# Half of the q and k transposes of two attention mixers moved from TensorE to VectorE and a round trip through HBM, and one projection order for both mixers

## The chip, the cores and the metric

The kernel runs on one core of a Trainium2 chip. The metric is the device time of one execution in microseconds (us). A profile of one execution accompanies each time: it tells what each engine did when, on TensorE (PE for matmuls, PEld for its weight loads), VectorE (DVE), ScalarE (ACT), GpSimd (POOL) and SyncE (SP, which here only issues transfers).

## The reference

A decoder trunk of two layers over 256 positions and 1024 channels, 16 heads of 64, in float32. Each layer is an FFN half-step, an attention mixer and another FFN half-step, all on normed input:

```python
for layer in range(2):
    h = h + 0.5 * swiglu(rmsnorm(h, ffn1_norm[layer]), ...)
    hn = rmsnorm(h, mix_norm[layer])
    if layer == 0:
        h = h + mixer_a(hn, a_w_qkv, a_w_o, pos)          # q, k, v from hn
    else:
        h = h + mixer_b(hn, b_w_q, b_w_o, k, v, ...)      # k, v from shared_kv
    h = h + 0.5 * swiglu(rmsnorm(h, ffn2_norm[layer]), ...)
    if layer == 0:
        k, v = shared_kv(h, kv_norm, kv_w, pos)
return rmsnorm(h, final_norm)
```

In both mixers q and k get a partial rotary turn (the first 16 of each head's 64 channels). At 256 positions mixer a is causal attention with weights that count how many of three dilated windows hold a key, and mixer b is plain causal attention; the kernel does both with the same code and two masks.

## The kernel before

Every float32 operand is split into a high part (float32r, by ACT) and the rest (by DVE), and a product takes three matmuls: high x high, high x low, low x high. Weights stream from HBM through a ring of five raw tiles and are split on ACT and DVE (`wh_`, `wl_`) a few pieces ahead of TensorE. The FFNs fill most of the time; the change is in `mixer`, called once per layer ("a", then "b").

A mixer projects the 256 tokens in two halves t = 0, 1 of 128 (tokens on partitions). `segs` lists the projections in order: each is up to 512 columns wide, and runs through `product` (L188, L190, L192). The heads go in four groups g of four heads (256 columns). `evacuate` brings a projection out of PSUM with the norm's scale (`rt_`, L1091), `rotate` turns the first channels on DVE (L910 to L913), and values are split to `vs_`. When q and k of a group and half are there, `turn_in` turns them on TensorE: four transposes of 128x128 against an identity (L1080) into a PSUM tile `qt_`, then `parts_of` splits it into `qk_` (ACT L99, DVE L96). `scores` (matmuls `s_`, L931 to L939), a softmax over ACT, DVE and POOL (`sm_`, `nm_`, `ls_`), the transposes of the weights (`pt_`, L971), `values` (`po_`, L1002) and the output projection (`ot_`, L877 to L879) follow.

The order of all this is the order of the program, set by an `Agenda`: projections advance a clock by 0.68 per step, and follow-up calls are entered with a delay on that clock (`agenda.after(1.5, ...)`, `soon` is 0.7). `plan` gives, per group, the delays of scores (s), transposes (t) and values (v; vt also does the next pair's transposes). A scheduler then puts each engine's instructions in a row. Within an engine instructions run in that row, and SP's transfers too are issued in one row.

The two mixers have different orders. Mixer a projects q and k of a group together, each group in turn:

```python
    qk = [(n1, xs, [("q", w, g * n, n, g), ("k", w, H * DH + g * n, n, g)]) for g in range(NG)]
    v = [(n1, xs, [("v", w, 2 * H * DH + g * n, 2 * n, g)]) for g in (0, 2)]
    mixer("a", [qk[0], v[0], qk[1], qk[2], qk[3], v[1]],
```

Mixer b projects k and v of group 0, q of groups 0 and 1, k and v of group 1, k of groups 2 and 3, q of 2 and 3, v of 2 and 3.

The last stage of the kernel (after mixer b) already turns data by another route, for the residual stream: DVE transposes 32x32 blocks (`turned`, L1196), SP writes the pieces to HBM (L1201) and reads them back in another order (`h`, L1207).

Of the kernel before, what the change touches and what calls it, by code (L numbers as in the profile page):

```python
# [10 lines left out]
F32 = mybir.dt.float32  # L11
# [56 lines left out]
def trunk(ctx: ExitStack, tc: tile.TileContext, a: dict, out: bass.AP):  # L68
# [14 lines left out]
    def atile(shape, dt=F32, name="a"):  # L83
        return ap_.tile(shape, dt, tag="a", name=name)
# [4 lines left out]
    def flat(ap):  # L89
        return ap.rearrange("p c n -> p (c n)")  # L90

    def parts_of(hi, lo, src, scale=1.0, later=None):

        def rest():
            if isinstance(scale, float):
                return first, nc.vector.tensor_sub(lo, src, hi.bitcast(F32))  # L96
            return first, nc.vector.scalar_tensor_tensor(lo, src, scale, hi.bitcast(F32), op0=ALU.mult, op1=ALU.subtract)

        first = nc.scalar.activation(hi, src, AF.Copy, scale=scale)  # L99
        (later or (lambda call: call()))(rest)  # L100
# [4 lines left out]
    def trt(name):  # L105
        return trp.tile([P, 512], F32, tag="tr", name=name)
# [796 lines left out]
    def rotate(v, t, name):  # L903

        n = v.shape[1]
        cs = rot[:, t, 0:1, :].to_broadcast([P, n, ROT])
        sn = rot[:, t, 1:2, :].to_broadcast([P, n, ROT])
        ta = sp.tile([P, n, ROT], F32, tag="rota", name=f"ra_{name}", bufs=2)
        tb = sp.tile([P, n, ROT], F32, tag="rotb", name=f"rb_{name}", bufs=2)
        nc.vector.tensor_mul(ta, v[:, :, :ROT], cs)  # L910
        nc.vector.tensor_mul(tb[:, :, :HALF], v[:, :, HALF:ROT], sn[:, :, :HALF])
        nc.vector.tensor_mul(tb[:, :, HALF:], v[:, :, :HALF], sn[:, :, HALF:])
        nc.vector.tensor_add(v[:, :, :ROT], ta, tb)  # L913
# [116 lines left out]

        return scores, turn, values, values_on

    def mixer(name, segs, plan, wo, mask, after, queue={}, beside=(), idle={}):

        n = HG * DH
        blocks, heads, qks, vss = [], {}, {}, {}
        specs = []  # L1040
# [24 lines left out]
        scores, turn, values, values_on = attention(agenda, lambda g: (qks[g], vss.get(g)), mask, name, blocks, idle)

        def turns(p):
            for i in range(2):
                turn(p, i)

        def turn_in(g, t):

            if t == 0:
                qks[g] = ap_.tile([P, 2, 4, NT, P], F32R, tag="qk", name=f"qk_{name}{g}", bufs=2)
            tr = trt(f"qt_{name}{g}_{t}")
            for i, kind in enumerate("qk"):
                s = heads[kind, g, t].rearrange("p a b -> p (a b)")
                for k in range(2):
                    at = (2 * i + k) * P
                    nc.tensor.transpose(tr[:, at:at + P], s[:, k * P:(k + 1) * P], ident)  # L1080
            parts_of(*[qks[g][:, i, :, t, :] for i in range(2)], tr.rearrange("p (k n) -> p k n", n=P), later=agenda.soon)
            if t == NT - 1:
                for wait, step, p in plan[g]:
                    agenda.after(wait, {"s": scores, "t": turns, "v": values, "vt": values_on}[step], p)

        def evacuate(i, t, r, ac, parts):
            at, turned = 0, []
            wide = sum(c for kind, _, _, c, _ in parts if kind != "v")
            if wide:
                rt = atile([P, wide // DH, DH], name=f"rt_{name}{i}_{t}")  # L1090
                nc.scalar.activation(flat(rt), ac[:, :wide], AF.Copy, scale=r)  # L1091
                agenda.soon(lambda: rotate(rt, t, f"{name}{i}_{t}"))
            for kind, _, _, c, first in parts:
                for j in range(c // n):
                    src = ac[:, at:at + n]
                    if kind == "v":
                        v = atile([P, HG, 2, DH], F32R, name=f"vs_{name}{first + j}_{t}")
                        vss.setdefault(first + j, []).append(v)
                        parts_of(v[:, :, 0], v[:, :, 1], src.rearrange("p (j d) -> p j d", d=DH), r, later=agenda.soon)
                    else:  # L1100
                        heads[kind, first + j, t] = rt[:, at // DH:at // DH + HG]
                        turned.append(first + j)
                    at += n
            for g in sorted(set(turned)):
                if ("q", g, t) in heads and ("k", g, t) in heads:
                    agenda.after(4.4 - 0.8 * t if i == 0 else 3.2, turn_in, g, t)

        def projections():
            for i, (norm, x, parts) in enumerate(segs):
                acs = [acc(f"{''.join(part[0] for part in parts)}_{name}{i}_{t}") for t in range(NT)]  # L1110
                for k0 in range(0, KD, 4):
                    for t in range(NT):
                        for k in range(k0, k0 + 4):
                            w = pieces[4 * i + k // 2][k % 2]
                            product([acs[t]], *x[t](k), [w], k == 0, k == KD - 1)
                            yield 0.68
# [41 lines left out]
    def ending(at, apart=2.6):  # L1158
        return [(at, "t", 4)] + [(at + apart * i + 2.1, "vt" if i < 3 else "v", 4 + i) for i in range(4)]

    mixer("a", [qk[0], v[0], qk[1], qk[2], qk[3], v[1]],
          [steps(0, 3.0, 11.0, 14.5, 16.5, 19.3), steps(1, 3.0, 11.0, 13.8, 16.5, 19.3), steps(2, 3.0),
           [(4.0, "s", (6, 7))] + ending(8.4)],
          a["a_w_o"][0], mask, n2, {3: 4, 4: 5}, beside=[lambda: None] * 2 + [f20.copy] * 12, idle={4: [f20.add] * 2, 8: [f20.add], 12: [f20.add], 16: [f20.add] * 3})
    calls_f20 = spaced([(at, f11) for at in range(4, 8)], [(1, f20)] + [(at, f11) for at in range(6, 10)])
    m20 = MadeSums("f20_d", a["ffn2_w_down"][0], (0, 3, 7))
    ffn("f20", 0, 2, n2, n3, fast=tuple(range(9)), queue=(6, 7) + (LAST_O,) * 6, kept=m20.kept | f20.kept,
# [13 lines left out]
    mixer("b", [kv[0], q[0], kv[1], k2, q[1], v2],  # L1181
          [joined_steps(0, 3.0, 11.0, 15.5, 19.8), joined_steps(1, 4.0, 12.4, 16.5, 20.7), [],
           steps(2, 2.2) + [(7.0, "s", (6, 7))] + ending(9.4, 2.7)],
          a["b_w_o"][0], mask, n6, {3: 4}, beside=[lambda: None] * 2 + [f21.copy] * 12, idle={4: [f21.add], 8: [f21.add] * 2, 16: [f21.add] * 3})
    m21 = MadeSums("f21_d", a["ffn2_w_down"][1], (0, 3))
    calls_f21 = spaced([], [(at, f21) for at in range(1, 7)])
    sums = left_sums(range(9), ("mk", "kx4", "kx6", "qk", "qk", "pT", "qk", "qk", "gf"))
# [113 lines left out]
```

## Time and profile before

| | |
|---|---|
| median of 3 runs | 946.78 us (lowest 945.91) |
| the profiled execution | 946.6 us, span of its instructions 944.8 us |
| busy, share of the span | PE 99%, PEld 86%, DVE 91%, ACT 70%, POOL 20% |
| DMA | 256 MB moved, 271 GB/s on the mean |
| granted TensorE clock | 0.999 |

One of the three runs took 1895.78 us, twice the others; the median is not touched by it. PE counts as busy from a matmul's start to its end, and matmuls overlap, so 99% tells that TensorE is never without work, not that it is at its peak. The span is the time from the first to the last instruction; 1.8 us of the execution lie around it. The chain of work that ended last tells which engine's time the end follows, and the windows of a stage tell what the other engines have free there.

### The profile page before, as it was taken

To read this page: it belongs to the slowest core of one execution; us is meant where nothing else is said; L and a number is where in the kernel's file an instruction comes from. 1 tells how busy PE (TensorE), PEld (TensorE's weight loads), DVE (VectorE), ACT (ScalarE), POOL (GpSimd) and SP (SyncE) were. 2 spreads that over 40 slices of the span, in tenths; PEclk is the share of its full clock that TensorE was granted. 3 is DMA by queue.
4 is the path that set the end of the run, shared out by engine and by line. 5 is a ranking of instruction groups with operands and counts; after the bars stand their busy time and mean duration, and the time that the engine had idled before them with its cause. 6 is when DMAs were issued, how large, how long until landed. Compare 5 with 4: busy or idle time off the path is not lost.

```text
span 944.8 us, 15060 instructions
## 1 busy us (share of the span) xinstructions
PE 936.8 (99%) x5250; PEld 811.1 (86%) x5250; DVE 858.0 (91%) x1552; ACT 658.8 (70%) x1157; POOL 193.0 (20%) x207
## 2 busy tenths in 40 slices
PE   9999999999999999999999999999999999999997
PEld 7888888888899888888888888888888988888886
DVE  7999989988888799989999998899889887999997
ACT  7766667766877756657786656887587875757773
POOL 0132100013641310200024320000253622330000
PEclk9999999999999999999999999999999999999999
DMA  9999778998489899968999986699959599999791
GB/s 321 361 357 337 202 273 284 351 320 216 121 208 258 268 329 278 256 179 326 346 322 315 318 250 191 217 362 380 341 188 223 156 256 263 280 204 312 253 370 45
DMA packets 170092, 255.98 MB, mean 271 GB/s; under 512 B 15520, under 2 KB 116128, under 8 KB 166560
## 3 DMA queue, kind: packets, MB, share of 16 engines
q1 hardware_dynamic: 157216, 226.05, 71.2%
q0 software_dynamic: 12224, 28.32, 15.5%
q8 instruction: 41, 0.67, 0.3%
q10 hardware_dynamic: 576, 0.66, 0.2%
q14 instruction: 35, 0.29, 0.1%
HBM read 241.36 MB, written 47.19 MB: 305 GB/s over the span
## 4 chain that ended last, share of the span: by engine, by line
PE 97%; DVE 1%; DMA 1%; ACT 0%; issue 0%; SPq 0%; POOLq 0%; POOL 0%; DVEq 0%; ACTq 0%
PE f_g L199 17%; PE f_u L199 17%; PE f_u L205 9%; PE f_g L205 9%; PE dn_f_d L190 4%; PE dn_f_d L188 4%; PE dn_f_d L192 4%; PE dn_f_d_m L190 3%; PE dn_f_d_m L192 3%; PE dn_f_d_m L188 3%; PE qk_a L188 2%; PE qk_a L192 2%; PE qk_a L190 2%; PE ot_bo L877 1%; PE v_a L188 1%; PE ot_bo L878 1%
## 5 line engine op out<-in xcount | busy, mean ns | idle before, releaser
L199 PE MATMUL f_g<-x_n,wh_f_g 128*128 128x512 f32 x672 | 170.4, 392 | 0.0
L199 PE MATMUL f_u<-x_n,wh_f_u 128*128 128x512 f32 x672 | 168.8, 390 | 0.0
L199 PEld LDWEIGHTS f_u<-x_n,wh_f_u 128*128 128x128 f32 x672 | 126.2, 188 | 26.5
L199 PEld LDWEIGHTS f_g<-x_n,wh_f_g 128*128 128x128 f32 x672 | 123.0, 188 | 23.7
L177 DVE TENSOR_TENSOR wl_f_u<-raw_f_u,wh_f_u 128x1024 fp32r<-128x1024 f32 x84 | 101.6, 1217 | 2.7 <-ACT wh_f_u L176 2.2
L177 DVE TENSOR_TENSOR wl_f_g<-raw_f_g,wh_f_g 128x1024 fp32r<-128x1024 f32 x84 | 101.5, 1216 | 1.3 <-ACT wh_f_g L176 1.0
L176 ACT ACTIVATE wh_f_u<-raw_f_u 128x1024 fp32r<-128x1024 f32 x84 | 87.8, 1051 | 13.3 <-PE f_g L199 10.0
L205 PE MATMUL f_u<-x_n,wl_f_u 128*128 128x256 f32 x672 | 96.7, 283 | 0.0
L205 PE MATMUL f_g<-x_n,wl_f_g 128*128 128x256 f32 x672 | 96.3, 282 | 0.0
L205 PEld LDWEIGHTS f_g<-x_n,wl_f_g 128*128 128x128 f32 x672 | 90.7, 191 | 4.0
L176 ACT ACTIVATE wh_f_g<-raw_f_g 128x1024 fp32r<-128x1024 f32 x84 | 86.6, 1050 | 4.6 <-DMA raw_f_g<-in_ffn_w_gate_dram 1.9
L205 PEld LDWEIGHTS f_u<-x_n,wl_f_u 128*128 128x128 f32 x672 | 87.6, 192 | 0.0
L640 POOL COPY scrap<-act_f 128x1 f32<-128x1 f32 x19 | 40.2, 2118 | 126.0 <-ACT act_f L99 112.2
L99 ACT ACTIVATE left<-q_f 128x512 fp32r<-128x512 f32 x35 | 22.0, 629 | 42.3 <-DVE q_f L417 42.3
L669 POOL DMA_DIRECT2D made_f_d<-made_f_d x44 | 26.5, 645 | 109.9 <-DVE made_f_d L664 26.2
L301 POOL TENSOR_TENSOR d_n<-w_n,expo 128x8 f32<-128x8 f32 x4 | 8.5, 2133 | 186.7 <-DVE w_n L297 186.7
L962 POOL TENSOR_SCALAR sm_b<-sm_b,ls_b 128x128 f32<-128x128 f32 (+1 forms) x32 | 33.7, 1069 | 31.8 <-DVE ls_b L960 31.8
L472 ACT ACTIVATE g_f<-g_f 128x512 f32<-128x512 f32 x30 | 19.0, 632 | 30.2 <-DVE g_f L471 30.0
L962 POOL TENSOR_SCALAR sm_a<-sm_a,ls_a 128x128 f32<-128x128 f32 (+1 forms) x32 | 32.9, 1047 | 34.1 <-DVE ls_a L960 19.6
L99 ACT ACTIVATE act_f<-g_f 128x256 fp32r<-128x256 f32 x60 | 21.7, 409 | 23.1 <-DVE g_f L475 23.0
L96 DVE TENSOR_TENSOR left<-q_f,left 128x512 fp32r<-128x512 f32 x35 | 23.9, 684 | 7.4 <-ACT left L99 7.4
L99 ACT ACTIVATE x_n<-gains_hT 128x256 fp32r<-128x256 f32 x48 | 21.8, 499 | 11.2 <-DVE gains_hT L830 8.6
(754 smaller groups left out, 2496.0 us busy)
## 6 DMA issues: line engine op xcount, KB each, us to landing
raw_f_g<-in_ffn_w_gate_dram SPq DMA_DIRECT2D x42, 1024.0 KB, 8.8
raw_f_u<-in_ffn_w_up_dram SPq DMA_DIRECT2D x42, 1024.0 KB, 7.9
raw_f_d<-in_ffn_w_down_dram SPq DMA_DIRECT2D x17, 1024.0 KB, 6.2
right_f_d<-in_ffn_w_down_dram SPq DMA_DIRECT2D x32, 512.0 KB, 9.3
raw_f_d<-in_ffn_w_down_dram SPq DMA_DIRECT2D x27, 512.0 KB, 5.1
made_f_d<-in_ffn_w_down_dram SPq DMA_DIRECT2D x44, 256.0 KB, 8.0
made_f_d<-made_f_d POOLq DMA_DIRECT2D x44, 256.0 KB, 6.3
right_f_d<-in_ffn_w_down_dram POOLq DMA_DIRECT2D x16, 512.0 KB, 8.3
```

The costliest lines, as they stand in the source:

```text
L96: return first, nc.vector.tensor_sub(lo, src, hi.bitcast(F32))
L99: first = nc.scalar.activation(hi, src, AF.Copy, scale=scale)
L176: nc.scalar.activation(wh, r, AF.Copy)
L177: nc.vector.tensor_sub(wl, r, wh.bitcast(F32))
L188: nc.tensor.matmul(ac, xh, wh, start=first, stop=False)
L190: nc.tensor.matmul(ac, xh, wl, start=False, stop=False)
L192: nc.tensor.matmul(ac, xl, wh, start=False, stop=last)
L199: nc.tensor.matmul(ac, wh, flat(x), start=first and i == 0, stop=False)
L205: nc.tensor.matmul(ac[:, :S], wl, x[:, 0, :], start=False, stop=last and i == len(ws) - 1)
L640: mark = nc.gpsimd.tensor_copy(scrap, latest[-1][:, 0, 0:1].bitcast(F32))
L669: nc.gpsimd.dma_start(self.home[:, j, n], part)
L962: done = nc.gpsimd.tensor_scalar(sm[:, seg], sm[:, seg], ls[:, t:t + 1], None, op0=ALU.mult)
```

## The change

Mixer a gets the projections and the plan of mixer b. In both mixers a table FAR names what no longer goes through TensorE: k of group 0, q of group 1, and k of groups 2 and 3, that is half of all q and k. For these, `turn_far` transposes the 32x32 blocks of a token half on DVE and writes the four blocks of 32 partitions to HBM, in pieces of 32 numbers (128 bytes), each at the place that its turned position has. After the second half one transfer reads the whole back as channels on partitions (`near_`, in the place called "gf"). `turn_near` splits it into `qk_`; `turn_in` transposes and splits only what is left. `turn_near` for group 0 is called before the second half's `turn_in`, for the other groups after it.

```diff
+    def turn_far(kind, g, m, rt, t):
+        if t == 0:
+            turning[kind, g] = aside.tile([m * n // Q, Q, NT, P], F32, tag=f"far_{name}{kind}{g}",
+                                          name=f"far_{name}{kind}{g}")
+        to = turning[kind, g]
+        part = atile([P, m * n], name=f"far_{name}{kind}{g}_{t}")
+        nc.vector.transpose(part, flat(rt))
+        for b in range(P // Q):
+            own = slice(b * Q, (b + 1) * Q)
+            nc.sync.dma_start(to[:, :, t, own].rearrange("c j i -> j c i"),
+                              part[own].rearrange("j (c i) -> j c i", i=Q))
+        if t == NT - 1:
+            whole = xp.tile([P, 2 * m, S], F32, tag="gf", name=f"near_{name}{kind}{g}")
+            nc.sync.dma_start(whole, to.rearrange("(k c) j t i -> (c j) k (t i)", c=P // Q))
+            for i in range(m):
+                fetched[kind, g + i] = whole[:, 2 * i:2 * i + 2].rearrange("p k (t i) -> p k t i", i=P)
+
+    def turn_near(g):
+        for i, kind in enumerate("qk"):
+            if (kind, g) in fetched:
+                parts_of(*[qks[g][:, part, 2 * i:2 * i + 2] for part in range(2)], fetched[kind, g], later=agenda.soon)
 ...
     def turn_in(g, t):
 ...
+        elif g == 0:
+            turn_near(g)
         tr = trt(f"qt_{name}{g}_{t}")
-        for i, kind in enumerate("qk"):
+        near = [kind for kind in "qk" if (kind, g) not in fetched]
+        for i, kind in enumerate(near):
 ...
         if t == NT - 1:
+            if g > 0:
+                agenda.after(0.7 * (g - 1), turn_near, g)
 ...
     (in evacuate, behind the call of rotate)
+                kind, first = parts[0][0], parts[0][4]
+                if (kind, first) in far:
+                    skip, m = far[kind, first]
+                    agenda.after(1.4, turn_far, kind, first + skip, m, rt[:, skip * HG:(skip + m) * HG], t)
 ...
-    mixer("a", [qk[0], v[0], qk[1], qk[2], qk[3], v[1]],
-          [steps(0, 3.0, 11.0, 14.5, 16.5, 19.3), steps(1, 3.0, 11.0, 13.8, 16.5, 19.3), steps(2, 3.0),
-           [(4.0, "s", (6, 7))] + ending(8.4)],
+    FAR = {("k", 0): (0, 1), ("q", 0): (1, 1), ("k", 2): (0, 2)}
+    mixer("a", [kv[0], q[0], kv[1], k2, q[1], v2],
+          [joined_steps(0, 3.0, 11.0, 15.5, 19.8), joined_steps(1, 4.0, 12.4, 16.5, 20.7), [],
+           steps(2, 2.2) + [(7.0, "s", (6, 7))] + ending(9.4, 2.7)],
```

TensorE in mixer b, at the first half of the last two groups (`qt_b`), between products of the v projection. Before:

```order
L192 MATMUL v_b_0_8037<-wh_vb_0_0_7884,x_kx_5636 128x512
L1080 MATMUL qt_b_0_8059<-ident,rt_b_0_7996 128x128 x2
L1080 MATMUL qt_b_0_8059<-ident,rt_b_0_7824 128x128 x2
L1080 MATMUL qt_b_0_8066<-ident,rt_b_0_7996 128x128 x2
L1080 MATMUL qt_b_0_8066<-ident,rt_b_0_7824 128x128 x2
L188 MATMUL v_b_0_8037<-wh_vb_0_1_7905,x_kx_5769 128x512
```

and now:

```order
L190 MATMUL v_b_0_8127<-wl_vb_0_0_7967,x_kx_5685 128x512
L192 MATMUL v_b_0_8127<-wh_vb_0_0_7966,x_kx_5685 128x512
L1107 MATMUL qt_b_0_8149<-ident,rt_b_0_8086 128x128 x2
L1107 MATMUL qt_b_0_8154<-ident,rt_b_0_8086 128x128 x2
L188 MATMUL v_b_0_8127<-wh_vb_0_1_7987,x_kx_5818 128x512
```

Four of the eight transposes, those of k, are gone.

SP's row of transfers in mixer b around the weights of k of groups 2 and 3 (`raw_kb`) and of q (`raw_qb`); `right_f_d` are copies within HBM for a later FFN. Before:

```order
L372 DMA raw_kb_0_7384<-in_kv_w_dram 128x4x512
L631 DMA right_f_d_126<-in_ffn_w_down_dram 256x1x512
L372 DMA raw_kb_4_7455<-in_kv_w_dram 128x4x512
L631 DMA right_f_d_126<-in_ffn_w_down_dram 256x1x512
L372 DMA raw_qb_0_7500<-in_b_w_q_dram 128x4x512
```

and now:

```order
L372 DMA raw_kb_0_7440<-in_kv_w_dram 128x4x512
L631 DMA right_f_d_126<-in_ffn_w_down_dram 256x1x512
L1082 DMA far_bk_7431<-far_bk_0_7432 32x8x32 x4
L1082 DMA far_bk_7431<-far_bk_1_7499 32x8x32 x4
L372 DMA raw_kb_4_7519<-in_kv_w_dram 128x4x512
L1086 DMA near_bk_7505<-far_bk_7431 128x2x256
L631 DMA right_f_d_126<-in_ffn_w_down_dram 256x1x512
L1082 DMA far_bq_7562<-far_bq_0_7563 32x8x32 x4
L372 DMA raw_qb_0_7571<-in_b_w_q_dram 128x4x512
```

The second half of the k weights and those of q now stand behind the short writes, which wait for DVE; the read of group 0's k (`near_bk`) waits for all eight writes.

DVE in mixer b ahead of the third scores (`sm_b`, `nm_b` are their first reduction, `wl_bo` a weight split, `oT_b` an attention output). Before:

```order
L390 TENSOR_TENSOR wl_bo_1_8195<-raw_bo_7955,wh_bo_1_8194 128x1024
L96 TENSOR_TENSOR qk_b_8058<-qt_b_1_8110,qk_b_8058 128x4x128
L96 TENSOR_TENSOR qk_b_8065<-qt_b_1_8116,qk_b_8065 128x4x128
L96 TENSOR_TENSOR oT_b_8127<-o_b_8096,oT_b_8127 128x256
L390 TENSOR_TENSOR wl_bo_0_8347<-raw_bo_8039,wh_bo_0_8346 128x1024
L949 ISA sm_b_0_8172,nm_b_0_8170<-s_b_0_8146,mask_7238 128x256
```

and now:

```order
L390 TENSOR_TENSOR wl_bo_0_8219<-raw_bo_8045,wh_bo_0_8218 128x1024
L96 TENSOR_TENSOR qk_b_8148<-qt_b_1_8196,qk_b_8148 128x2x128
L96 TENSOR_TENSOR qk_b_8153<-qt_b_1_8200,qk_b_8153 128x2x128
L96 TENSOR_TENSOR qk_b_8148<-near_bk_8015,qk_b_8148 128x512
L96 TENSOR_TENSOR oT_b_8209<-o_b_8182,oT_b_8209 128x256
L96 TENSOR_TENSOR qk_b_8153<-near_bk_8015,qk_b_8153 128x512
L390 TENSOR_TENSOR wl_bo_1_8280<-raw_bo_8045,wh_bo_1_8279 128x1024
L949 ISA sm_b_0_8257,nm_b_0_8255<-s_b_0_8231,mask_7287 128x256
```

The two splits of what TensorE turned are half as wide, and two splits of the fetched k stand behind them.

More of the change, by code (lines that the diff above doesn't have):

```diff
@@ L1031, in attention, with mixer @@
         return scores, turn, values, values_on
-    def mixer(name, segs, plan, wo, mask, after, queue={}, beside=(), idle={}):
+    def mixer(name, segs, plan, wo, mask, after, queue={}, beside=(), idle={}, far={}):
         n = HG * DH
         blocks, heads, qks, vss = [], {}, {}, {}
+        turning, fetched = {}, {}
         specs = []
@@ L1080, in turn_in @@
                     nc.tensor.transpose(tr[:, at:at + P], s[:, k * P:(k + 1) * P], ident)
-            parts_of(*[qks[g][:, i, :, t, :] for i in range(2)], tr.rearrange("p (k n) -> p k n", n=P), later=agenda.soon)
+            first = 2 * "qk".index(near[0])
+            own = slice(first, first + 2 * len(near))
+            parts_of(*[qks[g][:, i, own, t, :] for i in range(2)],
+                     tr[:, :2 * len(near) * P].rearrange("p (k n) -> p k n", n=P), later=agenda.soon)
             if t == NT - 1:
+                if g > 0:
+                    agenda.after(0.7 * (g - 1), turn_near, g)
                 for wait, step, p in plan[g]:
@@ L1146, in trunk @@
     w, n = a["a_w_qkv"][0], HG * DH
-    qk = [(n1, xs, [("q", w, g * n, n, g), ("k", w, H * DH + g * n, n, g)]) for g in range(NG)]
-    v = [(n1, xs, [("v", w, 2 * H * DH + g * n, 2 * n, g)]) for g in (0, 2)]
     def steps(g, first, *at):
@@ L1159, in ending @@
         return [(at, "t", 4)] + [(at + apart * i + 2.1, "vt" if i < 3 else "v", 4 + i) for i in range(4)]
-    mixer("a", [qk[0], v[0], qk[1], qk[2], qk[3], v[1]],
-          [steps(0, 3.0, 11.0, 14.5, 16.5, 19.3), steps(1, 3.0, 11.0, 13.8, 16.5, 19.3), steps(2, 3.0),
-           [(4.0, "s", (6, 7))] + ending(8.4)],
-          a["a_w_o"][0], mask, n2, {3: 4, 4: 5}, beside=[lambda: None] * 2 + [f20.copy] * 12, idle={4: [f20.add] * 2, 8: [f20.add], 12: [f20.add], 16: [f20.add] * 3})
+    kv = [(n1, xs, [("k", w, H * DH + g * n, n, g), ("v", w, 2 * H * DH + g * n, n, g)]) for g in range(2)]
+    q = [(n1, xs, [("q", w, g * n, 2 * n, g)]) for g in (0, 2)]
+    k2, v2 = [(n1, xs, [(kind, w, c0 + 2 * n, 2 * n, 2)]) for kind, c0 in (("k", H * DH), ("v", 2 * H * DH))]
+    FAR = {("k", 0): (0, 1), ("q", 0): (1, 1), ("k", 2): (0, 2)}
+    mixer("a", [kv[0], q[0], kv[1], k2, q[1], v2],
+          [joined_steps(0, 3.0, 11.0, 15.5, 19.8), joined_steps(1, 4.0, 12.4, 16.5, 20.7), [],
+           steps(2, 2.2) + [(7.0, "s", (6, 7))] + ending(9.4, 2.7)],
+          a["a_w_o"][0], mask, n2, {3: 4}, beside=[lambda: None] * 2 + [f20.copy] * 12, idle={4: [f20.add] * 2, 8: [f20.add], 12: [f20.add], 16: [f20.add] * 3}, far=FAR)
     calls_f20 = spaced([(at, f11) for at in range(4, 8)], [(1, f20)] + [(at, f11) for at in range(6, 10)])
@@ L1183, in trunk @@
            steps(2, 2.2) + [(7.0, "s", (6, 7))] + ending(9.4, 2.7)],
-          a["b_w_o"][0], mask, n6, {3: 4}, beside=[lambda: None] * 2 + [f21.copy] * 12, idle={4: [f21.add], 8: [f21.add] * 2, 16: [f21.add] * 3})
+          a["b_w_o"][0], mask, n6, {3: 4}, beside=[lambda: None] * 2 + [f21.copy] * 12, idle={4: [f21.add], 8: [f21.add] * 2, 16: [f21.add] * 3}, far=FAR)
     m21 = MadeSums("f21_d", a["ffn2_w_down"][1], (0, 3))
```

## The prediction

> **What bounds the kernel now.** I read the page's busy times and its chain of work first, then the waits of TensorE, then the two mixers' stretches beside a stretch that already turns data through HBM.
>
> ```profile
> PE   936.8 (99%) x5250; PEld 811.1 (86%) x5250; DVE 858.0 (91%) x1552; ACT 658.8 (70%) x1157; POOL 193.0 (20%) x207
> ...
> PE 97%; DVE 1%; DMA 1%; ACT 0%; issue 0%; SPq 0%; POOLq 0%; POOL 0%; DVEq 0%; ACTq 0%
> ```
> ```profile
> engine line waited for: us in total, times, longest us
> PE f_g L199 <- ACT wh L515: 0.8, 1, 0.8
> PE busy L124 <- PEq L1284: 0.8, 1, 0.8
> ```
> ```profile
> 181.00:284.00 103.00, 103.00 (x637) 88.48 (x636) 89.52 (x230) 77.77 (x169) 40.21 (x39) 1.00 0.80 227
> 660.00:752.00 92.00, 92.00 (x589) 79.76 (x588) 79.85 (x224) 69.66 (x161) 43.19 (x41) 1.00 0.76 227
> ```
> ```profile
> 790.00:800.00 10.00, 10.00 (x61) 8.92 (x60) 4.97 (x10) 4.25 (x10) 1.48 (x3) 1.00 1.06 356
> 830.00:845.00 15.00, 15.00 (x83) 13.07 (x82) 13.89 (x24) 9.80 (x19) 5.31 (x3) 1.00 1.06 224
> 800.00:850.00 50.00, 50.00 (x293) 44.46 (x292) 48.42 (x88) 31.31 (x56) 18.14 (x11) 1.00 1.03 243
> ```
> TensorE (PE) carries 97% of the chain and waits for another engine once, 0.8 us. In the window rows the columns are length, then busy time of PE, weight load, DVE, ACT and POOL, granted clock (1.00), DMA share, GB/s. In both mixers PE is busy for the whole stretch. So an instruction taken from PE there comes off the end, as long as nothing new makes PE wait. DVE has 13.5 of 103 and 12.2 of 92 us free, ACT 25.2 and 22.3, the 16 DMA engines 20% and 24%, about 21 and 22 us.
>
> **The PE transposes that go.** In each mixer 4 of the 8 pairs (q or k, group) leave PE: k of group 0, q of group 1, k of groups 2 and 3. Each pair is 2 token halves of 2 transposes: 16 of 32.
>
> ```profile
> L1080 PE MATMUL qt_b<-ident,rt_b x32: 270/272/273, 675.0 to 723.1; 128*128 128x128 f32 x32
> L99 ACT ACTIVATE qk_b<-qt_b x8: 574/592/600, 675.7 to 724.2; 128x512 fp32r<-128x512 f32 x8
> L96 DVE TENSOR_TENSOR qk_b<-qt_b,qk_b x8: 678/682/684, 677.4 to 725.4; 128x512 fp32r<-128x512 f32 x8
> ```
> ```profile
> 675.12 0.44 PE qt_b L1080 x4
> ...
> 718.10 0.87 PE qt_b L1080 x8
> ```
> 272 ns is the time of one transpose from end to end, but they are pipelined: on the chain (start, length) four take 0.44 us and eight 0.87, 0.109 each. 2 mixers x 16 x 0.109 = **3.5 us off PE**.
>
> **The first mixer's new order.** The trace has both orders side by side. From the first projection of each mixer to the first matmul of the FFN behind it:
>
> ```profile
> 183.99 0.39 PE L188 MATMUL qk_a<-wh_qka,x_n 128*128 128x512 f32 x1
> ...
> 295.26 0.40 PE L199 MATMUL f_g<-x_n,wh_f_g 128*128 128x512 f32 x1
> ```
> ```profile
> 650.94 0.39 PE L188 MATMUL kv_b<-wh_kvb,x_kx 128*128 128x512 f32 x1
> ...
> 761.90 0.40 PE L199 MATMUL f_g<-x_n,wh_f_g 128*128 128x512 f32 x1
> ```
> ```profile
> 194.34 0.46 PE col_n L259 x4
> ```
> That is 111.27 us against 110.96, and the first holds 0.46 us of norm products that the second has not. Both keep PE full, so the order is worth 0, give or take 0.3.
>
> **What is added beside PE.** Per mixer: four VectorE transposes of 128x256 and two of 128x512; the splits, which were 8 of 128x512 on ACT and DVE, become 8 of 128x256 and 4 of 128x512; SP issues 24 writes and 3 loads.
>
> ```profile
> L269 DVE STREAM_TRANSPOSE t_n<-ss_n x5: 434/435/439, 21.6 to 770.0; 128x256 f32<-128x256 f32 x5
> ```
> ```profile
> L1201 SPq DMA_DIRECT2D turned<-turned x16: 302/366/3722, 789.3 to 812.6; - x16
> L1207 SPq DMA_DIRECT2D h<-turned x16: 487/1372/4347, 818.6 to 843.5; - x16
> L1196 DVE STREAM_TRANSPOSE turned<-gains_hT x4: 669/704/708, 784.3 to 801.5; 128x512 f32<-128x512 f32 x4
> ...
> DMA to landing us min/median/max: 3.2/7.2/12.0
> ```
> ```profile
> L99 ACT ACTIVATE oT_b<-o_b x8: 401/418/421, 704.9 to 754.1; 128x256 fp32r<-128x256 f32 x8
> L96 DVE TENSOR_TENSOR oT_b<-o_b,oT_b x8: 411/418/420, 705.8 to 755.3; 128x256 fp32r<-128x256 f32 x8
> ```
> DVE: 4 x 0.435 + 2 x 0.704 = 3.1 us of transposes, and splits of 8 x 0.418 + 4 x 0.682 = 6.1 for 8 x 0.682 = 5.5. That is +3.8, against 12 to 13 free. ACT: 8 x 0.418 + 4 x 0.592 = 5.7 for 4.7, +1.0 against 22 free. The first mixer also gets ten rotations for eight, which I leave in its 13.5 free. On totals all of it lies beside PE; what counts is when the turned data arrive.
>
> **The new wait.** Scores of a group now need data that went DVE, HBM, SBUF, ACT, DVE. The nearest row for either hop is the kernel's own last stage above: 64 KB pieces land 3.2 to 12.0 us after issue, 7.2 in the median, but there the DMA share is 1.03, in the mixers 0.80 and 0.76. The lowest time of a write to HBM is that of the last stores (KB, us to landing):
>
> ```profile
> out_dram<-out SPq DMA_DIRECT2D x2, 256.0 KB, 2.1
> ```
> Against this stands the slack, read in the second mixer, whose order both will have: the end of the last rotation of the turned half, and the start of the scores that need it.
>
> ```profile
> 665.27 0.22 DVE L913 TENSOR_TENSOR rt_b<-ra_b,rb_b 128x64 f32<-128x64 f32 x1
> ...
> 676.04 0.30 DVE L913 TENSOR_TENSOR rt_b<-ra_b,rb_b 128x128 f32<-128x128 f32 x1
> ...
> 706.13 0.28 DVE L913 TENSOR_TENSOR rt_b<-ra_b,rb_b 128x128 f32<-128x128 f32 x1
> ```
> ```profile
> 682.16 0.97 PE L931 MATMUL s_b<-qk_b 64*128 64x256 f32 x12
> ...
> 696.92 0.97 PE L931 MATMUL s_b<-qk_b 64*128 64x256 f32 x12
> ...
> 726.05 0.97 PE L931 MATMUL s_b<-qk_b 64*128 64x256 f32 x12
> ```
> Slack is 16.7 us for k of group 0, 20.6 for q of group 1, 19.6 for k of groups 2 and 3. PE comes sooner by the transposes gone in between (4 x, 8 x and 8 x 0.109): 16.2, 19.7 and 18.8.
>
> The path for group 0: transpose 0.44, four issues of 0.37 to 0.49 (1.7), a write hop, one issue 0.4, a load hop, split 0.59 on ACT and 0.68 on DVE: 3.8 plus two hops. Two hops may thus take 12.4. For groups 2 and 3 the transpose is 0.70 and an issue has 512 pieces like h's, 0.49 to 1.37: 4.4 to 7.9 plus two hops, so they may take 10.9 to 14.4. Lower end 2.1 + 3.2 = 5.3: in time everywhere. Medians 14.4: late by 2.0 in group 0, in time in group 1, late by up to 3.5 in groups 2 and 3. Maxima 24.0: late by 11.6, 8.1 and 13.1. I take 5 us a hop, between lowest and median, since the queues have gaps here: **no wait for the data**.
>
> In the program an SP transfer also waits for the landing of the one eight before it, so these short writes, four by four, wait on each other and on the weights ahead of them; that is another reason to stay above the lowest hop. Queued behind a late landing would be, on SP, the next weights; on ACT, the weight splits behind the split of the fetched half; on PE, everything behind the scores. The SP rows in the order show the one load moved far:
>
> ```profile
> 658.10 0.38 SPq L372 DMA_DIRECT2D raw_kb<-in_kv_w_dram  x1
> ```
> ```profile
> 674.74 1.06 ACT L388 ACTIVATE wh_kb<-raw_kb 128x1024 fp32r<-128x1024 f32 x1
> ```
> ```profile
> raw_kb<-in_kv_w_dram SPq DMA_DIRECT2D x1, 1024.0 KB, 7.3
> ```
> It now follows eight writes, the last four ready at 665.5 + 0.44; issued at about 667.6 it lands at 674.9, when ACT wants it at 674.7. Cost 0.2 us on ACT, none on PE; with queues of the last stage's 12 us it would be 5 us, on ACT, which sits free for 24% of the stretch.
>
> One place is tight without any late landing. Before the third scores of the second mixer:
>
> ```profile
> 724.82 1.28 DVE L96 TENSOR_TENSOR qk_b<-qt_b,qk_b 128x512 fp32r<-128x512 f32 x2
> ```
> The splits end at 726.10, as the scores (726.05) reach their low parts. DVE then did two of 0.68 there; now it does two of 0.42 and, behind them, the fetched halves' two of 0.68, with group 2's first. PE arrives 0.9 sooner. I charge 0.3 us a mixer, between 0 and 1.2 (two splits of 0.68 less what starts earlier): **+0.6**.
>
> **DMA time.** 8192 pieces of 128 bytes are written per mixer. In 830 to 845 the same share of DMA time moved 224 GB/s instead of the 356 of 790 to 800: 37% of 15 us, 5.6 us, went to some 4096 pieces of 128 bytes (8 of h's 16 transfers, 512 each). So the estimate is 11 us per mixer, in 21 to 22 free. These pieces are read; no row of before writes such pieces. The bounds are nothing and twice that, 22 us, where the gaps would be gone and the hops be those of the loaded stage: the first rival. I take 11, the only row.
>
> The Trainium skill, "DMA: Bandwidth & Descriptors", Specifications, asks for at least 512 B, since below that the engine does a read-modify-write. It speaks for the upper bound; the trace of before can't settle it.
>
> **The sum.** The profiled execution took 946.6 us, 1.8 beside its 944.8 span; the median of the runs is 946.78, 0.2 above. 946.6 - 3.5 + 0.6 + 0 = **943.7**.
>
> **Rivals.**
> 1. *Slower: the hops are late.* From 12.4 us for two hops on, scores wait and PE with them. At the medians 2.0 + 3.5 = 5.5 us a mixer, 11.0 in all: 946.6 - 3.5 + 11.0 = 954.1. At the maxima 32.8 a mixer: 1008.7. For it: the median row, and the copies of right_f_d (512 KB, HBM to HBM) between the writes on SP. Against: the DMA gaps in the mixers.
> 2. *DVE becomes the bound before scores.* Both mixers pay 1.2 at the third scores: 946.6 - 3.5 + 2.4 = 945.5. For it: the splits that end with nothing to spare; against: DVE's free 12 us.
> 3. *The change doesn't do what it says*, the transposes' PE time being hidden under weight loads: 946.6. Against: 0.87 to 0.44, exactly in proportion.
>
> The Trainium skill, same page, Rules for kernel authors, says not to transpose by a plain DMA with a rearranged access pattern, which it puts 19 times behind the hardware's own. Here the turning inside 32x32 is DVE's and the pieces are 128 bytes; 37% lost in the stage that does so is far from 19 times. By the rule the case is the far end of rival 1.
>
> **Chances and range.** Forecast 0.58 (942.5 to 944.9), rival 1 0.22, rival 2 0.15, rival 3 0.05. Low end 942.3: all 3.5 us, the order's 0.3 and a spread of 0.5. Rival 1 spreads from 947 to 1008, half of it under 951, so 942.3 to 951 leaves out about 0.15. Two per cent, what a measurement here can tell from no change, is 19 us: faster by that needs six times the transposes removed, 0.01; slower needs 22 us of waits, a third of what the maxima in rival 1 give, 0.03; within 0.96.
>
> **What would show it.** Right: PE transposes of q and k 16 per mixer; PE still without waits in 181 to 284 and 660 to 752; both mixers 1.7 us shorter from first projection to FFN; landings of the far and near transfers under 6 us. Wrong: PE waiting at the score lines for qk of ACT or DVE, ACT idle before the split of a near tile with a DMA as releaser, SP waiting for landings ahead of weight loads.

## The result: 0.7% slower, and the profile after

The changed kernel takes 952.77 us in the median against 947.04 us of the kernel before: a ratio of 1.0069, 95% interval 1.0057 to 1.0081. (Ratios here and below are worked out over all runs but that of 1895.78 us, and not from the two medians.) I had forecast 943.7, in 942.3 to 951.0. The profiled execution took 951.99 us, with a span of 950.2.

The page's busy row and its chain of work come first, then the four rows of TensorE that bound the mixers' stretches, as in the prediction:

```profile
PE 938.1 (99%) x5218; PEld 809.1 (85%) x5218; DVE 864.8 (91%) x1580; ACT 661.6 (70%) x1167; POOL 193.8 (20%) x207
...
PE 87%; DVE 3%; ACT 3%; DMA 2%; POOL 2%; issue 2%; POOLq 0%; SPq 0%; DVEq 0%; ACTq 0%
```
```profile
183.73 0.39 PE L188 MATMUL kv_a<-wh_kva,x_n 128*128 128x512 f32 x1
...
300.81 0.40 PE L199 MATMUL f_g<-x_n,wh_f_g 128*128 128x512 f32 x1
...
656.30 0.39 PE L188 MATMUL kv_b<-wh_kvb,x_kx 128*128 128x512 f32 x1
...
767.68 0.40 PE L199 MATMUL f_g<-x_n,wh_f_g 128*128 128x512 f32 x1
```
The 32 matmuls are gone (5250 to 5218), and yet TensorE holds 87% of the chain instead of 97%. The first mixer takes 117.08 us (111.27 before), the second 111.39 (110.96); what lies outside them is 0.8 us shorter in all. So the first mixer lost 5.8 us, the second 0.4, and both should have gained 1.75 from the transposes, less the 0.3 that I charged.

TensorE's waits from 184 to 300 us name the place: the `pt` transposes of the softmax, which the prediction did not speak of.

```profile
PE pt_a L971 <- POOL sm_a L962: 3.7, 4, 1.4
PE pt_a L971 <- DVE nm_a L949: 0.2, 1, 0.2
PE qt_a L1107 <- DVE rt_a L913: 0.2, 1, 0.2
```
In order of time (start, length, and in brackets the idle time before it and its releaser), with two rows of windows (length, then busy PE, PEld, DVE, ACT, POOL, granted clock, DMA share, GB/s):

```profile
242.73 0.39 PE L192 MATMUL q_a<-wh_qa,x_n 128*128 128x512 f32 x1
243.69 0.33 PE L971 MATMUL pt_a<-ident,sm_a 128*128 128x128 f32 x1 [0.57 <-POOL sm_a L962]
244.58 0.44 PE L971 MATMUL pt_a<-ident,sm_a 128*128 128x128 f32 x2 [0.57 <-POOL sm_a L962]
246.14 0.33 PE L971 MATMUL pt_a<-ident,sm_a 128*128 128x128 f32 x1 [1.12 <-POOL sm_a L962]
247.87 0.69 PE L971 MATMUL pt_a<-ident,sm_a 128*128 128x128 f32 x2 [1.40 <-POOL sm_a L962]
...
249.21 0.63 PE L192 MATMUL q_a<-wh_qa,x_n 128*128 128x512 f32 x1
249.64 0.63 PE L188 MATMUL q_a<-wh_qa,x_n 128*128 128x512 f32 x1
```
```profile
243.00:248.00 5.00, 1.35 (x6) 0.61 (x6) 4.47 (x7) 1.85 (x3) 5.00 (x6) 0.94 1.07 170
248.00:251.00 3.00, 3.00 (x9) 2.44 (x10) 0.56 (x1) 0.49 (x1) 3.00 (x5) 0.52 0.95 356
```
Six transposes stretch over 5 us, with four waits for GpSimd (POOL) to scale the next piece of `sm`. Behind them projections start every 0.43 us instead of 0.23: the granted clock is 0.52 for 3 us. The six projections that start from 248.21 on take 2.7 us until the next one at 250.89, where six at 0.23 take 1.4: 1.3 us more.

GpSimd's own timeline, before and after:

```profile
210.22 9.61 POOL L962 TENSOR_SCALAR sm_a<-sm_a,ls_a 128x128 f32<-128x128 f32 x8 [13.49 <-DVE ls_a L960]
219.77 1.11 POOL L636 DMA_DIRECT2D right_f_d<-in_ffn_w_down_dram  x1
227.32 1.06 POOL L636 DMA_DIRECT2D right_f_d<-in_ffn_w_down_dram  x1 [6.44 <-issue]
237.78 8.72 POOL L962 TENSOR_SCALAR sm_a<-sm_a,ls_a 128x128 f32<-128x128 f32 x8 [9.40 <-DVE rt_a L913]
```
```profile
220.63 9.09 POOL L962 TENSOR_SCALAR sm_a<-sm_a,ls_a 128x128 f32<-128x128 f32 x8 [24.16 <-PE kv_a L192]
229.66 1.13 POOL L636 DMA_DIRECT2D right_f_d<-in_ffn_w_down_dram  x1
239.85 1.06 POOL L636 DMA_DIRECT2D right_f_d<-in_ffn_w_down_dram  x1 [9.05 <-DVE oT_a L96]
240.46 10.26 POOL L962 TENSOR_SCALAR sm_a<-sm_a,ls_a 128x128 f32<-128x128 f32 x8
```
Behind the fourth scaling the `idle` argument of the first mixer puts two calls of `f20.add`: DMAs that GpSimd issues and that add to `right_f_d` in HBM (L636, "accumulating transfers" below). For the first of each pair, the trace gives from issue to landing, before and after:

```profile
DMA to landing us min/median/max: 7.2/7.2/7.2
```
```profile
DMA to landing us min/median/max: 9.8/9.8/9.8
```
The first transfers, issued at 219.77 and 229.66, thus land at 227.0 and 239.5, and the second ones are issued at 227.32 and 239.85, some 0.3 us after that each time. So the second waits for the first one's landing, and all that stands behind it in GpSimd's queue waits too. Before, the next scalings came 10.5 us behind the second transfer's issue. The new order brings the first group 10.4 us later and leaves the second where it was, so the queue is held when the scalings' turn comes. The "DVE oT_a" in the row's bracket is only what ended last by the profile; the constant 0.3 us is the better witness.

### The profile page after: what moved, and what is told of

It reads as the page before. It is cut to its first block, busy times and chain, and to the rows that moved or that the text cites. A ratio compares the mean times of both kernels' runs of the same rounds, so it can differ in the third digit from the quotient of the medians.

```text
span 950.2 us, 15134 instructions
## 1 busy us (share of the span) xinstructions
PE 938.1 (99%) x5218; PEld 809.1 (85%) x5218; DVE 864.8 (91%) x1580; ACT 661.6 (70%) x1167; POOL 193.8 (20%) x207
## 4 chain that ended last, share of the span: by engine, by line
PE 87%; DVE 3%; ACT 3%; DMA 2%; POOL 2%; issue 2%; POOLq 0%; SPq 0%; DVEq 0%; ACTq 0%
PE f_g L199 16%; PE f_u L199 16%; PE f_u L205 8%; PE f_g L205 8%; PE dn_f_d L190 4%; PE dn_f_d L192 4%; PE dn_f_d L188 4%; PE dn_f_d_m L190 3%; PE dn_f_d_m L192 3%; PE dn_f_d_m L188 3%; DMA raw_f_u<-in_ffn_w_up_dram 1%; ACT sm_a L955 1%; PE kv_b L188 1%; POOL sm_a L962 1%; PE kv_b L192 1%
## 5 line engine op out<-in xcount | busy, mean ns | idle before, releaser
L640 POOL COPY scrap<-act_f 128x1 f32<-128x1 f32 x19 | 36.9, 1944 | 129.4 <-ACT act_f L99 115.6
L962 POOL TENSOR_SCALAR sm_b<-sm_b,ls_b 128x128 f32<-128x128 f32 (+1 forms) x32 | 36.4, 1156 | 25.1 <-DVE ls_b L960 25.1
L406 ACT ACTIVATE u_f<-f_u 128x256 f32<-128x256 f32 x60 | 22.1, 383 | 11.9 <-PE f_u L205 11.8
```

Source lines behind the costliest of these rows:

```text
L640: mark = nc.gpsimd.tensor_copy(scrap, latest[-1][:, 0, 0:1].bitcast(F32))
L962: done = nc.gpsimd.tensor_scalar(sm[:, seg], sm[:, seg], ls[:, t:t + 1], None, op0=ALU.mult)
```

## The experiments

The theories that the expectations name. **Q**: GpSimd's queue, as above. **O**: the new order itself is too tight. **V**: VectorE's 32x32 transposes hold back the softmax. **L**: the last scores' way to the `pt` transposes sets the end anyway. **H**: the way through HBM puts the splits of fetched halves too late. **D**: the transfers themselves.

All times are medians in us; each ratio is to runs of the kernel before on the same chip. "Mixers" is the first and second stretch, first projection to first FFN matmul, in the one profiled execution; it is free of what varies elsewhere. Where the second mixer is unchanged (before, e1, e4, e12), it took 110.93 to 110.96, so differences of some 0.1 can be read.

| run | time | before | ratio (95%) | mixers |
|---|---|---|---|---|
| before | | | | 111.27 + 110.96 = 222.23 |
| the change | 952.77 | 947.04 | 1.0069 (1.0057 to 1.0081) | 117.08 + 111.39 = 228.47 |
| e1_order_only | 946.58 | 946.32 | 1.0001 (0.9989 to 1.0014) | 111.56 + 110.96 = 222.52 |
| e2_far_b_only | 946.86 | 946.32 | 1.0003 (0.9994 to 1.0011) | 111.25 + 111.69 = 222.94 |
| e3_adds_apart | 947.47 | 946.32 | 1.0011 (1.0003 to 1.0020) | 111.94 + 111.63 = 223.57 |
| e4_order_adds_apart | 947.09 | 946.32 | 1.0012 (1.0000 to 1.0024) | 111.32 + 110.93 = 222.25 |
| e5_unturned | 943.66 | 946.17 | 0.9974 (0.9964 to 0.9984) | 109.59 + 109.21 = 218.80 |
| e6_no_k2 | 945.63 | 946.17 | 0.9994 (0.9985 to 1.0003) | 111.21 + 110.63 = 221.84 |
| e7_k2_later | 945.79 | 946.17 | 1.0003 (0.9994 to 1.0013) | 111.22 + 110.97 = 222.19 |
| e8_extra_dve | 946.94 | 946.17 | 1.0015 (1.0005 to 1.0025) | 111.94 + 110.91 = 222.85 |
| e9_unturned_dve | 945.06 | 946.33 | 0.9984 (0.9967 to 1.0000) | 110.25 + 109.59 = 219.84 |
| e10_unturned_dve_hbm | 945.12 | 946.33 | 0.9985 (0.9970 to 1.0001) | 110.20 + 109.95 = 220.15 |
| e11_k3_later | 944.24 | 946.33 | 0.9973 (0.9961 to 0.9985) | 110.75 + 110.02 = 220.77 |
| e12_three_adds | 954.15 | 946.33 | 1.0085 (1.0059 to 1.0111) | 118.09 + 110.96 = 229.05 |
| e13_hbm_no_dve | 945.02 | 946.83 | 0.9986 (0.9977 to 0.9994) | 109.99 + 111.51 = 221.50 |
| e14_k3_early | 944.92 | 946.83 | 0.9978 (0.9968 to 0.9987) | 111.09 + 109.77 = 220.86 |

### Where the first mixer's 5.8 us went

**e1_order_only**: `far=FAR` is left out of both calls of `mixer`.

> The changed kernel with every q and k turned by TensorE again; only the first mixer's new order is left of the change. Theory Q (the second of the two accumulating transfers behind the fourth scaling waits in GpSimd's queue for the first one to land, and the second group of scalings waits behind it; the turning's transfers made that landing take 9.8 us instead of 7.2): with no turning transfers the first one lands some 7 us after its issue, about when the second group is ready, so most of the loss goes: 946 to 949 us. Theory O (the new order by itself has too little slack before TensorE's pt transposes): about 950 to 953 us. Theory V (VectorE's 32x32 transposes hold back the softmax): 946.5 to 947.5 us.

The order alone costs nothing (1.0001). Without turning transfers the first accumulating transfer lands after 7.1 us, and the second group of scalings starts in time by a hair:

```profile
230.28 1.10 POOL L636 DMA_DIRECT2D right_f_d<-in_ffn_w_down_dram  x1
237.73 1.06 POOL L636 DMA_DIRECT2D right_f_d<-in_ffn_w_down_dram  x1 [6.34 <-issue]
238.34 10.71 POOL L962 TENSOR_SCALAR sm_a<-sm_a,ls_a 128x128 f32<-128x128 f32 x8
```
Theory O falls. Q and V both stand.

**e3_adds_apart**, and **e4_order_adds_apart**, the same edit without `far=FAR`:

```
-idle={4: [f20.add] * 2, 8: [f20.add],     12: ...
+idle={4: [f20.add],     8: [f20.add] * 2, 12: ...
```

> The changed kernel with one of the two accumulating transfers behind the first mixer's fourth scaling put behind the eighth (the second mixer's table has it so). Theory Q: the second group of scalings starts about 2.1 us sooner and TensorE's wait of 3.7 us and the fall of its clock behind it mostly go: 947 to 949.5 us. Theories O and V: at most 0.5 us off, 952 to 953 us.

> The new order alone (all turning by TensorE) with the accumulating transfers apart as in the run before this one. Theory Q and theory V: 946.5 to 947.5 us, no difference from the kernel before. Theory O: over 949 us.

One transfer moved by four scalings takes back most of the loss, 1.0069 to 1.0011. The scalings now follow directly on the reciprocals (238.83 for 240.46), and the wait at `pt_a` falls from 3.7 to 0.5 us:

```profile
229.73 1.13 POOL L636 DMA_DIRECT2D right_f_d<-in_ffn_w_down_dram  x1
238.83 9.67 POOL L962 TENSOR_SCALAR sm_a<-sm_a,ls_a 128x128 f32<-128x128 f32 x8 [7.97 <-DVE ls_a L960]
```
e4, the order alone, is at 1.0012 (1.0000 to 1.0024).

**e12_three_adds** is the dose: in e1, three accumulating transfers behind the fourth scaling (`4: [f20.add] * 3`) and none behind the eighth.

> The new order alone (TensorE turns everything, 946.58 us) with three accumulating transfers behind the first mixer's fourth scaling instead of two, and none behind the eighth. Theory Q: each waits for the one before it to land, some 7.4 us apart (issues at 230, 237.7 and 245), so the second group of scalings starts at about 245.5 instead of 238.3 us, and with the fall of TensorE's clock behind the wait the time is 952 to 957 us. If the queue is not what costs: 946 to 947.5 us.

```profile
229.71 1.10 POOL L636 DMA_DIRECT2D right_f_d<-in_ffn_w_down_dram  x1
237.31 1.06 POOL L636 DMA_DIRECT2D right_f_d<-in_ffn_w_down_dram  x1 [6.50 <-issue]
244.62 0.93 POOL L636 DMA_DIRECT2D right_f_d<-right_f_d  x1 [6.25 <-DVE wl_va L390]
245.22 6.43 POOL L962 TENSOR_SCALAR sm_a<-sm_a,ls_a 128x128 f32<-128x128 f32 x8
```
The transfers are issued 7.6 and 7.3 us apart, the scalings start at 245.2, and the time is 954.15 us: the numbers that Q gave, without any turning. Q is shown.

### Where the 3.5 us of TensorE went

With the queue mended, the whole change still gives no gain (e3: 1.0011), and the second mixer had none to begin with:

**e2_far_b_only**: the first mixer of the kernel before, the second of the changed one.

> The kernel before with the second mixer's turning alone; the first mixer is as it was. Nothing is changed ahead of 540 us. My forecast's sum would be 945.3 us (1.75 us of TensorE off, 0.3 us back). The trace of the changed kernel has the second mixer's stretch 0.43 us longer than before, so theories Q, O and V all expect 947.0 to 948.0 us; below 946 us would say that the second mixer lost its gain through what the first mixer had changed.

946.86, a little under the 947.0 to 948.0 expected, but no gain: the second mixer's loss is not inherited from the first. The next runs take the path apart, all with the transfers apart.

**e5_unturned**: `turn_far` makes nothing, and `turn_near` splits the unturned rows (`heads`) that are at hand.

> With the accumulating transfers apart, as in the next three runs. The 32 transposes of TensorE are off and nothing takes their place: the same halves of q and k are split from their rows as they are, unturned (so this kernel computes other scores), with no VectorE transposes and no way through HBM. Theory V (the 3.8 us of transposes that VectorE got in each mixer, in a stretch where it is busy 95% of the time, give the gain back): 943.0 to 944.5 us, the forecast's 3.5 us under the 947.09 of the run with the new order and transfers apart. Theory L (the last scores' way through VectorE, ScalarE and GpSimd to the pt transposes is as long as before, so what TensorE saves ahead of it becomes a wait): 946 to 947.5 us.

**e9_unturned_dve**: as e5, with `nc.vector.transpose(part, flat(rt))` back, its result unused.

> The kernel with unturned halves (other scores, no way through HBM, TensorE's 32 transposes off: 943.66 us), and VectorE's 32x32 transposes are made again in their places, their results not used. Theory V by VectorE's work: 945.0 to 947.0 us, most of the 3.5 us given back here. Theory H (what gives it back is the way through HBM: the split of the fetched halves stands later in ScalarE's and VectorE's order than that of halves at hand, just ahead of the third scores): 943.3 to 944.5 us.

**e10_unturned_dve_hbm**: as e9, with the writes and loads back, the loaded tile unused.

> As the run before this one, and the turned blocks are also written to HBM and fetched again, but the fetched tiles are not used (the split still reads the unturned rows: other scores). Theory V: as the run before it, 945 to 947 us. A theory D that the 96 transfers themselves (SyncE's issues ahead of the weights' loads, the DMA engines' time) give the gain back: 1 us or more over the run before it. Theory H: 943.5 to 944.7 us, since the splits stay where they are.

In the mixers' stretches: e4 to e5, TensorE's transposes off, -3.45. e5 to e9, VectorE's transposes, +1.04. e9 to e10, the transfers (54, not the 96 of my expectation), +0.31. e10 to e3, the fetched tiles used, +3.42. So L falls, and D, with 0.31 where it asked for 1 or more. Put back in this order, V takes 1.0 and the use of the fetched halves 3.4; e13 below shows that the order matters. By the medians alone e9 and e10 (945.06 and 945.12) lie in the range that V gave and above that of H. (The profiled execution of e9 lost 5.7 us behind the second mixer; its stretches are read alone.)

**e8_extra_dve**: as e4, with the transposes made and unused.

> TensorE turns everything as in the run with the new order and transfers apart (947.09 us), and VectorE's 32x32 transposes are made too, in their places, but their results are not used and nothing goes to HBM. This is the price of VectorE's 3.8 us per mixer by itself. Theory V: 949 to 951 us. Theory L: 947 to 948 us.

1.0015 beside e4's 1.0012, and 222.85 in the mixers beside 222.25: VectorE's extra work costs 0.6 us at most while TensorE keeps its own, far from the 949 to 951 that V gave. It costs more, 1.0, where TensorE has gained on it (e9).

**e13_hbm_no_dve**: e3 without VectorE's transposes (`part = flat(rt)`); the fetched tiles are used.

> Accumulating transfers apart; the rows of the far halves go through HBM as they are, without VectorE's 32x32 transposes (so the blocks arrive unturned inside and the scores are others), and the fetched tiles are used, with their splits in the late place. In the two mixers' stretches together (222.2 us before, 220.1 with the unused way through HBM, 223.6 with everything): theory H expects 222.0 to 223.0 us here and 946.0 to 947.2 us in all; theory V expects 219.0 to 220.5 us and 943.5 to 945 us.

At 221.50 (and 945.02 in all) it lies between H and V: neither alone gives the whole gain back. Against e5, V alone takes 1.04 (e9), the way through HBM with its late splits alone 2.70 (e13), both together 4.77 (e3). Taken off from the whole, V is worth 2.07 (e3 to e13). So V has 1.0 to 2.1 of the 4.8, depending on the order in which the parts are counted, and is no minor part. The ratios say the same: 0.9974 for e5, 0.9984 and 0.9986 with one of the two, 1.0011 with both, each to about 0.001.

The two mixers of e13 part: the first is 0.4 over e5, the second 2.3. Their rows of ScalarE and TensorE ahead of the third scores show a difference. First mixer:

```profile
251.39 0.65 ACT L99 ACTIVATE qk_a<-qt_a 128x256 fp32r<-128x256 f32 x2
251.92 0.64 ACT L99 ACTIVATE qk_a<-near_ak 128x512 fp32r<-128x512 f32 x1
253.72 0.77 ACT L1009 ACTIVATE o_a<-po_a 64x256 f32<-64x256 f32 x2 [1.16 <-PE po_a L1002]
254.52 0.63 ACT L99 ACTIVATE qk_a<-near_ak 128x512 fp32r<-128x512 f32 x1
...
257.57 0.97 PE L931 MATMUL s_a<-qk_a 64*128 64x256 f32 x12
```
Second mixer:

```profile
721.08 0.66 ACT L99 ACTIVATE qk_b<-qt_b 128x256 fp32r<-128x256 f32 x2
721.62 0.42 ACT L99 ACTIVATE oT_b<-o_b 128x256 fp32r<-128x256 f32 x1
721.93 1.15 ACT L99 ACTIVATE qk_b<-near_bk 128x512 fp32r<-128x512 f32 x2
...
723.02 1.35 PE L931 MATMUL s_b<-qk_b 64*128 64x256 f32 x12
```
Where the splits of the fetched k stand 5.7 and 3.1 us ahead of the scores, they cost 0.4; where they end as the scores begin, the twelve products take 1.35 us for 0.97, VectorE's softmax steps start behind them, and the stretch loses 2.3 (0.5 of it before these scores, which start 73.85 us into the mixer for 73.35 in e5). In e3, with VectorE's transposes, the second of these splits stands close ahead of the scores in the first mixer too, and both mixers are about 2.4 over e5. Not all of that is lost there: at the start of the third scores e3 is already 1.5 behind e5 in the first mixer and 0.7 in the second, so 0.85 and 1.7 go from there on. This is H by the rows of one kernel; the two mixers differ in other things too, so the place is strongly indicated rather than isolated.

**e6_no_k2** (`FAR` without `("k", 2)`), **e7_k2_later** (the third transposes planned 1.6 later), **e11_k3_later** and **e14_k3_early** (`("k", 2): (1, 1)`: of that pair only group 3, later and not).

> Only the first group's k and the second group's q go by VectorE and HBM; the k of groups 2 and 3 (half of the turned amount) stay with TensorE. Theory V, with the price at the k of groups 2 and 3, whose 128x512 transposes stand ahead of the reciprocals of the second softmax: 945.0 to 946.0 us. Theory L: 946.5 to 947.5 us.

> The transposes of the k of groups 2 and 3 are planned 1.6 us later, so that three of the four reciprocals of the second softmax stand ahead of them in VectorE's order. Theory V with the price in that place: 0.7 to 1.5 us under the 947.47 us of the run with transfers apart, 946.0 to 946.8 us. Theory V by VectorE's total work, and theory L: 947 to 948 us.

> A candidate: accumulating transfers apart, the transposes of the third way planned 1.6 us later, and of the k of groups 2 and 3 only that of group 3 goes by VectorE and HBM (its scores come some 5 us after group 2's). 24 of the 32 transposes are off TensorE, 2.6 us. Theories V and H both have less to take back here: 944.0 to 945.5 us. 946 us or more would say that neither place is what costs.

> The candidate (944.24 us) with the transposes of group 3's k back at their first delay of 1.4 us instead of 3.0, ahead of the reciprocals of the second softmax; they are 128x256 here and take 0.44 us instead of 0.71. Theory H: the choice of the group is what counts, 944.0 to 944.9 us. Theory V with the price in that place: 945 to 946 us.

These place the loss. Group 0's k and group 1's q (16 transposes off, 1.74 us) bring 0.41: e6 against e4. Adding group 3's k (e11) brings 1.07, all that its 8 transposes are worth (0.87) and 0.2 that is not explained: its scores come 6.3 us after group 2's, so its split has time. Adding group 2's k as well (e7) costs 1.42 where 0.87 should have come off. Planning the transposes earlier, ahead of the second softmax's reciprocals, costs 1.38 for both groups (e3 against e7) and 0.1 for one (e14 against e11). VectorE's row in the changed kernel shows that place:

```profile
237.42 0.71 DVE L1079 STREAM_TRANSPOSE far_ak<-rt_a 128x512 f32<-128x512 f32 x1
238.06 0.31 DVE L960 RECIPROCAL ls_a<-ls_a 128x2 f32<-128x2 f32 x4
```
**e11 is the best version**: 944.24 us, 0.9973 (0.9961 to 0.9985), for the change's 1.0069.

## Why the prediction was wrong, step by step

- *3.5 us off PE*: right. e4 to e5 measured 3.45 in the stretches; the third rival (hidden under weight loads) falls.
- *The first mixer's new order worth 0, give or take 0.3*: **the step that failed**. By itself the new order held (e1: +0.29). But I compared two mixers' orders on PE alone and called them one. Their `idle` tables differ: the first has two accumulating transfers behind the fourth scaling, the second one. The window row that I quoted has GpSimd busy for 40 of 103 us; I never read what stood in its queue. With the turning's longer landing (9.8 for 7.2 us) it cost 4.9 us, 228.47 to 223.57. My sum let TensorE wait only for the turned data, and had no term for a wait on GpSimd. With the queue mended, e3's 947.47 is still 3.8 over the forecast; the two terms below that were mis-sized account for that.
- *DVE's 3.8 us beside PE, at nothing*: mis-sized. The transposes cost 1.04 once PE was faster (e9), 2.07 counted from the whole (e3 to e13), and 0.6 at most while PE was not faster (e8). Free time summed over a stretch hid that none lay ahead of the reciprocals, where their place alone was worth 1.38 (e3 to e7).
- *No wait for the data, 5 us a hop*: right on the landings, which were mostly faster: the loads took 2.7 to 5.7 us, the writes 1.5 to 7.1. Of the second mixer's `far_bk` writes and `near_bk` loads together:

```profile
DMA to landing us min/median/max: 1.7/2.4/5.7
```
  No split waited for a landing. But TensorE paid for the splits' place. Ahead of the first scores of the first mixer, the load of `near_ak` landed 2.8 us after its issue, at 210.9; its split stands behind a weight split on ACT, at 214.13, and the scores stand in two pieces with three projections between them:

```profile
208.09 0.38 SPq L1086 DMA_DIRECT2D near_ak<-far_ak  x1
214.13 0.61 ACT L99 ACTIVATE qk_a<-near_ak 128x512 fp32r<-128x512 f32 x1
215.07 0.50 PE L931 MATMUL s_a<-qk_a 64*128 64x256 f32 x4
...
216.40 0.74 PE L931 MATMUL s_a<-qk_a 64*128 64x256 f32 x8
```
  I had read the slack as time for the hops, with the splits right behind them. In e13, where this split stands ahead of the weight splits, at 208.93, the scores stand in one piece. Measured from the first projection, e3, which has the two pieces, is 0.45 us behind e10 after these scores and 0.9 at the `pt` transposes that follow; e13 is level with e10 there.
- *The weights' load moved far, 0.2 us on ACT*: nothing by the load. It was issued at 673.84 and landed 5.5 us later, at 679.3. The split that wants it starts at 681.01, 24.7 us into the second mixer (681.01 less 656.30) for 23.8 before, behind other work in ACT's row; neither ACT nor PE waits for the load.

```profile
681.01 1.05 ACT L388 ACTIVATE wh_kb<-raw_kb 128x1024 fp32r<-128x1024 f32 x1
```
- *0.3 us a mixer at the third scores*: a right place, mis-sized, and not the only one. From e10 to e3 3.42 us went, 1.7 a mixer. From the start of the third scores on, e3 lost 0.85 and 1.1 against e10 in the two mixers, within the 1.2 that I had as a bound but far over the 0.3 in the sum; the splits delay not the scores alone but the softmax behind them, up to the third `pt` transposes. Another 0.9 went in the first mixer, from its first scores to the `pt` transposes behind them, and 0.6 in the second mixer ahead of its third scores, where I had charged nothing.
- *DMA time 11 us a mixer*: close. In windows of 108 us the share rose from 0.81 (e5, and e9 as well) to 0.90 (e10), 9.7 us, and it cost 0.31 in time (e9 to e10):

```profile
649.00:757.00 108.00, 108.00 (x687) 94.09 (x687) 95.51 (x261) 85.56 (x193) 45.81 (x42) 1.00 0.81 242
```
```profile
649.50:757.50 108.00, 107.77 (x681) 93.28 (x680) 97.24 (x264) 84.85 (x192) 45.31 (x42) 1.00 0.90 266
```
  The rule on pieces under 512 B (the Trainium skill, "DMA: Bandwidth & Descriptors", Specifications) had no price beyond these 0.31 us here. The 19-fold rule (the Trainium skill, same page, Rules for kernel authors) compares with a hardware transpose that no run here uses.
- *The sum with measured terms*: 946.6 - 3.45 + 1.04 + 0.31 + 3.42 + 4.9 + 0.02 (e4's order) = 952.8; the profiled execution took 952.0, and the 0.8 between them lies outside the mixers.
- *Rivals*: the first gave 954.1, near the result, by a mechanism that did not happen: no split waited for a landing, so the nearness is luck. The second (VectorE's splits ahead of the third scores, 945.5) happened, and is some 2.0 of the 4.8 us that are given back with the queue mended.

## What to carry to other kernels

When an order of work moves, list for every engine what else stands in its queue at that place, above all a DMA that waits for another one's landing: it holds every instruction behind it, on an engine that is busy only 20% of the time. Work taken off the bounding engine paid here only where its replacement ended well ahead of its consumer; take first the pieces whose consumer comes latest (here 24 of 32 transposes gained 2.1 us by the medians and all 32 nothing). And read an operation's slack in its place in the order, not from the free time of a stretch.

## What the runs showed of the hardware

**GpSimd beside VectorE.** In the kernel before, the eight scalings of `sm_b` behind the second scores, and the eight behind the third, with the same shapes (min, median, max in ns):

```profile
L962 POOL TENSOR_SCALAR sm_b<-sm_b,ls_b x8: 594/1072/1988, 704.5 to 712.1; 128x128 f32<-128x128 f32 x4, 128x256 f32<-128x256 f32 x4
```
```profile
L962 POOL TENSOR_SCALAR sm_b<-sm_b,ls_b x8: 592/756/917, 730.6 to 735.7; 128x128 f32<-128x128 f32 x4, 128x256 f32<-128x256 f32 x4
```
Beside the first group VectorE runs four 128x1024 subtractions of weights, both inputs in SBUF; beside the second none. The Trainium skill, "SBUF — State Buffer", Who interferes with whom, says that a VectorE instruction with two SBUF inputs contends with a GpSimd instruction that reads SBUF, and one with at most one SBUF input, outside its two-port modes, does not. These rows agree, though the two stretches differ in other things too: the DMA share is 0.45 in the first and 0.07 in the second. I had taken GpSimd's scaling as fixed.

**TensorE's clock** fell to 0.52 for 3 us behind 5 us in which it was busy for 1.35 (rows above), and in e12 to half:

```profile
249.00:251.00 2.00, 2.00 (x7) 1.61 (x7) 0.56 (x1) 0.49 (x1) 2.00 (x4) 0.50 1.15 220
```
The Trainium skill, "TensorE: Matmul & The Clock Gate", What's actually happening, has the clock halve after an idle window of about 3.4 us and return after a busy one. The half and the some 3 us agree. In the changed kernel, though, the longest single wait was 1.4 us, with six short transposes between the waits: a stretch that is mostly idle was enough.
